# Order of the output projection of a hybrid RWKV-7 / short-convolution block: M2 behind M1, one M1 block through a projection buffer, P4 among the second half's M1, sums and forms spread, end reordered

## The chip, the cores and the metric

The kernel runs on one core of one Trainium2 chip. A core has TensorE (matrix products; its weight loads are listed apart as PEld), VectorE (DVE), ScalarE (ACT), GpSimd (POOL) and SyncE (SP, which here only starts transfers), and 16 DMA engines between HBM and the core's SBUF. The metric is the device time of one execution in microseconds (us). The time before is the median of three runs, 1017.98 us (1017.09 to 1019.04).

## The reference

Inputs are `x` (512 rows of 2048), 16 meta rows put ahead of it, and weights. One layer:

```python
hn = _rmsnorm(h_res, norm_in_g[l])
P = hn @ w_in[l]                         # 2048 -> 4224 + 4096 columns
...
y = _rwkv7_recurrence(rh, decay, kh, vh, kk, kk * ah)     # 16 heads x 64, in chunks of 64 rows
y_a = (yn + bonus.reshape(bsz, L, D_RWKV)) * jax.nn.silu(g_r)
y_b = Bg * _causal_depthwise_conv(Cg * hc, conv_w[l]) * jax.nn.silu(g_c)
mix = jnp.concatenate([y_a, y_b], axis=-1)                # 1024 + 1024 columns
h_res = h_res + mix @ w_out[l]                            # 2048 x 2048
out = _rmsnorm(h_res, norm_f_g)
return out[:, N_META:]
```

The change is in the last three lines: the product of `mix` with `w_out`, the addition of `x` and the final RMSNorm.

## The kernel before

**Stages.** The input projection (L319 to L340) fills TensorE for most of the span; between its matmuls stand the chunk matrices of the recurrence, the recurrence itself (`recur`, L939) and the elementwise work. All products are made in three passes of a high and a low part (`hi`, `lo`): each float32 operand is split, ScalarE casting `hi` and VectorE (for some weights GpSimd) subtracting to get `lo`.

**Output product.** `mix` (four tiles `mix[0..3]` of 128 x 4 x 512, transposed) times `w_out` is computed in two halves of the output's columns. In each half a 2 x 2 block scheme in the manner of Strassen and Winograd makes seven products, named M1, M2, M7, Q6, P5, P4 and M3, in place of eight. Their left operands are parts of `mix` (M1: `mix` of the RWKV half and the first 256 rows, M2: the convolution half and the first 256 rows, P4: the convolution half and the last 256 rows) or *forms* S1, S3, S4, S5 of sums (L1112 `sums(q)`: four operations of 128 x 1024 on VectorE, for q = 0 and 1; L1155 `split_form`: the split of one form, a cast and a subtraction of 128 x 1024; eight of them). Their right operands are blocks of `w_out` (128 x 1024, 512 KB) or sums of blocks. Each product has four blocks g = 0..3 over the summed dimension.

**Units.** A unit `(half, product, g)` is 12 matmuls of 128 x 512: two row parts `s`, two parts `q` of the block, three passes. `units` (L1164) lists all 56 in TensorE's order, and TensorE follows it by hand. Before the change, each half is: M1 (g 0 to 3), then P5, M7, M3, Q6 for each g, then P4 and M2, interleaved in the first half, M2 last in the second. `split_unit` (L1205) makes a unit's right operand: two casts and two subtractions (tiles `o`, six buffers in the pool tag `w`, so up to three units ahead). After a product's last unit `close` (L1247) adds its PSUM banks to the tiles `xa` (first half) and `xb` (second), which also hold `x`; after Q6 six such additions use an SBUF tile `sh`, and when a tile is final, `squares` on ScalarE makes its part of the sum of squares and `gain` on GpSimd multiplies it by the final gain.

**Loads.** `chain[g]` (tiles `X0..X3`) gets its first `w_out` block by `begin_chain` (L1187) or, for g 0 to 2 of the first half, in the projection's weight stream; other blocks are added onto it by a transfer from GpSimd's queue (`add_by_transfer`, L1198) or by VectorE (`add`, L1201). `request` (L1192) loads one block into one of three `raw` buffers that the projection used for its weights. The tiles of the output stage in pool `pw`, `X3` among them, are available when the projection's memory is released (`ph1.close()`, L1142).

**What sets the order.** `at(u, fn, ...)` (L1279) hangs a helper in front of unit u of the list. On VectorE, ScalarE, GpSimd and SP a scheduler orders the work from there and each engine then runs its list strictly in order; the last part of the program (L1374 on) is ordered by hand on VectorE, ScalarE and GpSimd. SP's transfers leave in SP's order: one that waits for its buffer holds up those behind it. The lists around the change:

```python
for half in range(2):
    units += [(half, "M1", g) for g in range(4)]
    units += [(half, prod, g) for g in range(4) for prod in ("P5", "M7", "M3", "Q6")]
    ends = ("P4", 0), ("P4", 1), ("M2", 0), ("P4", 2), ("M2", 1), ("P4", 3), ("M2", 2), ("M2", 3)
    units += [(half, prod, g) for prod, g in sorted(ends, key=lambda e: half and e[0] == "M2")]
```

**End.** The last product (M2 of the second half) is made as bank `end` for rows 0 to 127 and as two banks of 256 columns for rows 128 to 255. `finish` (L1396) scales rows of a tile and stores them, `row_scale` (L1389) makes the row's factor (with a power on GpSimd), `finish_last` (L1408) scales and stores the last four tiles.

Of the kernel before, what the change touches and what calls it, by code (L numbers as in the profile page):

```python
# [9 lines left out]
F32 = mybir.dt.float32  # L10
# [3 lines left out]
ALU = mybir.AluOpType  # L14
# [63 lines left out]
def hymba_kernel(ctx: ExitStack, tc: tile.TileContext, xt, xtok, front, w_in, w_out, pv, lup, cst, msk, gf, out):  # L78
# [1033 lines left out]
    def sums(q):  # L1112
        a11, a21, a12, a22 = quarter(0, T0, q), quarter(0, T1, q), quarter(1, T0, q), quarter(1, T1, q)
        nc.vector.tensor_tensor(out=a22, in0=a22, in1=a21, op=ALU.subtract)
        nc.vector.tensor_tensor(out=a21, in0=a11, in1=a21, op=ALU.subtract)
        nc.vector.scalar_tensor_tensor(out=a11, in0=a22, scalar=-1.0, in1=a11, op0=ALU.mult, op1=ALU.subtract)
        nc.vector.scalar_tensor_tensor(out=a12, in0=a11, scalar=-1.0, in1=a12, op0=ALU.mult, op1=ALU.subtract)
# [16 lines left out]
    for j in range(NPAIR + 4, KT):  # L1134
# [3 lines left out]
        split_mix(j)  # L1138
    for _ in flow:
        pass  # L1140
    prefetch(len(stream))
    ph1.close()  # L1142
# [21 lines left out]
    units = []  # L1164
    for half in range(2):
        units += [(half, "M1", g) for g in range(4)]
        units += [(half, prod, g) for g in range(4) for prod in ("P5", "M7", "M3", "Q6")]
        ends = ("P4", 0), ("P4", 1), ("M2", 0), ("P4", 2), ("M2", 1), ("P4", 3), ("M2", 2), ("M2", 3)
        units += [(half, prod, g) for prod, g in sorted(ends, key=lambda e: half and e[0] == "M2")]
    U = {unit: u for u, unit in enumerate(units)}  # L1170
    right, straight = {}, {}
# [10 lines left out]
    def rows_of(half, k, col, g):  # L1182
        return w_out[2 * half + col, 4 * k + g]

# [4 lines left out]

    def request(half, k, col, g):  # L1192
        t = wp.tile([P, 1024], F32, tag="raw", name=f"wo{half}{k}{col}{g}", bufs=3)
        state["dma"] = nc.sync.dma_start(t, rows_of(half, k, col, g)).ins
        straight[half, k, col, g] = t

# [320 lines left out]
```

## Time and profile before

| | us |
|---|---|
| median of three runs | 1017.98 (1017.09 to 1019.04) |
| the profiled execution's own time | 1016.83 |
| its span on the page | 1015.1 |
| output stage: first M1 weights to the end of the span | 846.62 to 1015.1 |
| first-half block (P5, M7, M3, Q6) starts | 859.55 |
| second half's first P5 starts | 939.28 |
| first and last store issued | 1001.18 and 1010.72 |

The page gives busy time by engine; since TensorE's row is nearly full throughout, it tells little about what can be saved. More is read from the timeline of one engine: each row is a run of equal instructions (start, time until the last one's end, engine, line, operation, output and input, count), and in brackets the idle time just before it and the event that ended it. PEld rows are used for TensorE because a weight load starts only when its operand is there, and because the recorded ends of matmuls are modelled. In the names of tiles buffer numbers are left out: `o` is a split right operand, `S` a form, `m` a part of `mix`, `w` a split weight of the projection's stream, `wo` a raw `w_out` block, `x` a chain tile.

### The profile page before, as it was taken

What the parts mean: (1) busy time and instruction counts of PE and PEld (TensorE: products, weight loads), DVE (VectorE), ACT (ScalarE), POOL (GpSimd) and SP (SyncE); (2) the same over time, 40 slices, a digit from 0 to 9 for tenths busy, and PEclk for the clock granted to TensorE, in tenths of its full rate; (3) what the DMA queues carried; (4) which work ended last, traced back from release to release, by engine and by line L of the source; (5) the groups of instructions that cost most, each with busy time, mean ns of one, the idle gap of its engine ahead of it and who ended that gap; (6) DMA issues with size and microseconds to landing.
All of it is one profiled execution on the core that took longest, in us unless ns stands there. A gap on an engine that the chain in (4) does not pass through costs nothing.

```text
span 1015.1 us, 23761 instructions
## 1 busy us (share of the span) xinstructions
PE 995.6 (98%) x9723; PEld 913.6 (90%) x9723; DVE 684.3 (67%) x1305; ACT 393.9 (39%) x729; POOL 276.2 (27%) x292
## 2 busy tenths in 40 slices
PE   9999999999999999999999999999999999999996
PEld 8899998999988999998999998889898897787875
DVE  7677955587775568654668654244555697998787
ACT  7553423344323433323434323222222335545453
POOL 0122323233232323222423222223332332015001
PEclk9999999999999999999999999999999999999999
DMA  9525576446664363864273956977673698696754
GB/s 325 158 75 140 127 193 172 120 119 149 160 167 134 100 176 87 220 166 118 83 172 95 222 140 188 342 241 229 220 211 88 196 264 190 171 330 139 174 124 166
DMA packets 185037, 174.83 MB, mean 172 GB/s; under 512 B 121568, under 2 KB 142816, under 8 KB 184416
## 3 DMA queue, kind: packets, MB, share of 16 engines
q1 hardware_dynamic: 182336, 164.40, 56.3%
q0 software_dynamic: 2304, 8.39, 5.0%
q8 instruction: 76, 1.25, 0.5%
q10 hardware_dynamic: 288, 0.52, 0.1%
q14 instruction: 33, 0.27, 0.1%
HBM read 136.92 MB, written 36.35 MB: 171 GB/s over the span
## 4 chain that ended last, share of the span: by engine, by line
PE 55%; DVE 8%; DMA 3%; issue 2%; ACT 1%; SPq 0%; POOL 0%; DVEq 0%; ACTq 0%; POOLq 0%
PE ps_gc L328 8%; PE ps_B L328 7%; PE ps_h L328 7%; PE ps_C L328 6%; PE ps_v L328 5%; PE ps_k L328 5%; PE ps_g L328 4%; PE ps_r L328 4%; DVE o L1213 3%; DMA wo<-in_w_out_dram 2%; PE M L1240 2%; PE zy L1009 1%; PE zs L1005 1%; PE g L680 1%; DVE xb L1221 1%
## 5 line engine op out<-in xcount | busy, mean ns | idle before, releaser
L134 ACT CAST w<-wr 128x512 fp32r<-128x512 f32 x252 | 153.2, 618 | 292.7 <-PE ps_k L328 45.8
L135 POOL TENSOR_TENSOR w<-wr,w 128x512 fp32r<-128x512 f32 x119 | 166.6, 1400 | 362.0 <-ACT w L134 310.6
L135 DVE TENSOR_TENSOR w<-wr,w 128x512 fp32r<-128x512 f32 x133 | 94.3, 715 | 104.7 <-ACT w L134 99.6
L328 PE MATMUL ps_k<-xh,w 128*128 128x256 f32 (+1 forms) x512 | 95.6, 284 | 1.1 <-DVE w L135 1.1
L328 PE MATMUL ps_r<-xh,w 128*128 128x256 f32 (+1 forms) x512 | 95.7, 282 | 0.0
L328 PE MATMUL ps_v<-xh,w 128*128 128x272 f32 (+1 forms) x512 | 95.1, 283 | 0.0
L328 PE MATMUL ps_h<-xh,w 128*128 128x258 f32 (+1 forms) x512 | 94.1, 282 | 0.0
L328 PE MATMUL ps_C<-xh,w 128*128 128x258 f32 (+1 forms) x512 | 93.2, 281 | 0.0
L328 PE MATMUL ps_g<-xh,w 128*128 128x258 f32 (+1 forms) x512 | 92.2, 281 | 0.0
L328 PE MATMUL ps_B<-xh,w 128*128 128x512 f32 x256 | 83.4, 394 | 0.0
L328 PEld LDWEIGHTS ps_k<-xh,w 128*128 128x128 f32 x512 | 80.5, 190 | 1.6 <-DVE w L135 1.4
L328 PE MATMUL ps_gc<-xh,w 128*128 128x512 f32 x256 | 81.4, 393 | 0.3 <-DVE w L135 0.3
L328 PEld LDWEIGHTS ps_r<-xh,w 128*128 128x128 f32 x512 | 80.5, 189 | 0.2
L328 PEld LDWEIGHTS ps_h<-xh,w 128*128 128x128 f32 x512 | 79.7, 189 | 0.7
L328 PEld LDWEIGHTS ps_v<-xh,w 128*128 128x128 f32 x512 | 80.1, 189 | 0.3
L328 PEld LDWEIGHTS ps_C<-xh,w 128*128 128x128 f32 x512 | 79.6, 189 | 0.6
L328 PEld LDWEIGHTS ps_g<-xh,w 128*128 128x128 f32 x512 | 79.4, 189 | 0.5
L328 PE MATMUL ps_k<-xl,w 128*128 128x272 f32 (+1 forms) x256 | 73.1, 286 | 0.0
L328 PE MATMUL ps_h<-xl,w 128*128 128x256 f32 (+1 forms) x256 | 72.0, 281 | 0.6 <-issue 0.6
L328 PE MATMUL ps_v<-xl,w 128*128 128x256 f32 (+1 forms) x256 | 72.5, 283 | 0.0
L328 PE MATMUL ps_r<-xl,w 128*128 128x256 f32 (+1 forms) x256 | 72.3, 282 | 0.0
L328 PE MATMUL ps_g<-xl,w 128*128 128x256 f32 (+1 forms) x256 | 72.2, 282 | 0.0
(321 smaller groups left out, 2278.0 us busy)
## 6 DMA issues: line engine op xcount, KB each, us to landing
wr<-in_w_in_dram SPq DMA_DIRECT2D x126, 512.0 KB
ct<-opd SPq DMA_DIRECT2D x64, 288.0 KB
wo<-in_w_out_dram SPq DMA_DIRECT2D x24, 512.0 KB
x<-in_w_out_dram POOLq DMA_DIRECT2D x16, 512.0 KB, 6.2
opd<-ar SPq DMA_DIRECT2D x8, 576.0 KB
opd<-gt SPq DMA_DIRECT2D x16, 288.0 KB
opd<-bt SPq DMA_DIRECT2D x64, 64.0 KB
x<-in_w_out_dram SPq DMA_DIRECT2D x8, 512.0 KB
```

The lines of the kernel that those rows point to most:

```text
L134: nc.scalar.copy(hi, rq)
L135: low[q] = eng.tensor_tensor(out=lo, in0=rq, in1=hi.bitcast(F32), op=ALU.subtract).ins
L328: nc.tensor.matmul(ps[r], ww[:, w], xx[:, kt, a:b], start=(kt == 0 and n == 0), stop=(kt == KT - 1 and n == 2))
L680: nc.tensor.matmul(z[h][:, c - c0], bk[hs, c, h : h + 2, :].rearrange("p a s -> p (a s)"), ar[hs, c].rearrange("p a s -> p (a s)"), start= ...
L1005: nc.tensor.matmul(d[hs, j], w, x[hs], start=(a == 0), stop=(a == b - 1))
L1009: nc.tensor.matmul(d[ho, j], t[hs, o : o + CH], x[hs], start=(a == 0), stop=(a == b - 1))
L1213: nc.vector.tensor_tensor(out=lo, in0=rq, in1=hi.bitcast(F32), op=ALU.subtract)
L1221: nc.vector.tensor_tensor(out=h, in0=h, in1=ps, op=op)
L1240: nc.tensor.matmul(bank[s], left(prod, jj, m, s), w, start=(jj == 0 and n == 0), stop=(jj == 7 and n == 2))
```

## The change

The list of units becomes: half 0's M1 and then M2 (units 0 to 7); the block P5, M7, M3, Q6 four times (8 to 23); P4 g 0 to 2, then the second half's M1 g 0, P4 g 3, M1 g 1 to 3 (24 to 31); the second half's block (32 to 47); its P4 and M2 (48 to 55). The number of units and matmuls is the same. `request` moves ahead of `ph1.close()`, and M1's fourth block of the first half is requested there into a `raw` buffer; its chain tile is loaded later, for its other uses. The forms and sums hang on other units, `sums(1)` now as four separate operations. In the end part one `finish` of tile (0, 3) goes behind the last addition and one `gain` of a quarter behind `row_scale`.

```diff
@@ sums, before ph1.close() @@
-    def sums(q):
+    def sums(q, which=range(4)):
...
+        for n in which:
+            if n < 2:
+                o, x = ((a22, a22), (a21, a11))[n]
+                nc.vector.tensor_tensor(out=o, in0=x, in1=a21, op=ALU.subtract)
+            else:
+                o, x = ((a11, a22), (a12, a11))[n - 2]
+                nc.vector.scalar_tensor_tensor(out=o, in0=x, scalar=-1.0, in1=o, op0=ALU.mult, op1=ALU.subtract)
...
     prefetch(len(stream))
+    straight = {}
+    request(0, 0, 0, 3)
     ph1.close()
@@ units @@
+    def block(half):
+        return [(half, prod, g) for g in range(4) for prod in ("P5", "M7", "M3", "Q6")]
+
+    units = [(0, prod, g) for prod in ("M1", "M2") for g in range(4)] + block(0)
+    units += [(0, "P4", 0), (0, "P4", 1), (0, "P4", 2), (1, "M1", 0), (0, "P4", 3)]
+    units += [(1, "M1", g) for g in range(1, 4)] + block(1) + [(1, prod, g) for prod in ("P4", "M2") for g in range(4)]
@@ what hangs on which unit @@
+    at(0, split_unit, (0, "M1", 3), passing(0, 0, 0, 3))
+    at(2, begin_chain, 0, 3)
     for half in range(2):
-        o = 28 * half
         for g in range(4):
-            b = o + 4 + 4 * g
-            if half == 0:
-                if g == 3:
-                    at(-1, begin_chain, 0, g)
-                    at(0, split_unit, (0, "M1", g), chained(g))
-            else:
-                at(o + g - 4, begin_chain, 1, g)
-                at(o + g - 2, split_unit, (1, "M1", g), chained(g))
-            at(max(o + g, b - 5), add_by_transfer, half, 0, 1, g)
+            b, m1, m2 = U[half, "P5", g], U[half, "M1", g], U[half, "M2", g]
+            if half:
+                at(m1 - 4, begin_chain, 1, g)
+                at(m1 - 2, split_unit, (1, "M1", g), chained(g))
+            at(max(m1 + (half == 0 and g == 3), b - 5), add_by_transfer, half, 0, 1, g)
...
-            if half == 0:
-                at(U[half, "M2", g] - 4, request, 0, 1, 0, g)
-                at(U[half, "M2", g] - 2, split_unit, (0, "M2", g), passing(0, 1, 0, g))
+            if half:
+                at(m2 + 2 * g - g - 11, load_home, g)
             else:
-                at(o + 13 + 2 * g, load_home, g)
+                at(m2 - 5, request, 0, 1, 0, g)
+                at(m2 - 2, split_unit, (0, "M2", g), passing(0, 1, 0, g))
     for n, f in enumerate(("S1", "S3", "S4", "S5")):
-        at(n, split_form, f, 0)
-        if n == 2:
-            at(n + 1, sums, 1)
-        at(6 + n, split_form, f, 1)
+        at((1, 2, 4, 5)[n], split_form, f, 0)
+        at(6 + n, sums, 1, (n,))
+        at((10, 11, 13, 14)[n], split_form, f, 1)
@@ end @@
             squares(1, 2, part)
-            gain(1, 2, nc.vector, cols)
             if part == 0:
-                finish(0, (2, 0, 3))
+                gain(1, 2, nc.vector, cols)
+                finish(0, (2, 0))
                 nc.vector.tensor_tensor(out=fv[:, 1, 0:1], in0=fv[:, 1, 0:1], in1=ssq[:, 1, 3:4], op=ALU.add)
+        finish(0, (3,))
         row_scale(1, 4, nc.vector)
+        gain(1, 2, nc.vector, slice(256, 512))
         finish_last(1)
```

How the instructions stand is settled by a scheduler, so the lists of three places are shown. In the names, `o3_0` is part 0 of unit 3's right operand, `wo0103` the raw block of half 0, second row group, first column group, g 3; `x03` is the chain tile of half 0, g 3; `S101` the low part of form S1 for q = 0.

VectorE where the first half of the output begins, from the last split of `mix` on; before:

```order
L1114 TENSOR_TENSOR mix3_10658<-mix3_10658,mix1_10656 128x4x256
L1160 TENSOR_TENSOR S101_11293<-mix2_10657,S100_11292 128x1024
L1160 TENSOR_TENSOR S301_11289<-mix0_10655,S300_11288 128x1024
L1213 TENSOR_TENSOR o3_0_11315<-x03_11312,o3_0_11315 128x512
L1213 TENSOR_TENSOR o3_1_11318<-x03_11312,o3_1_11318 128x512
L1213 TENSOR_TENSOR o4_0_11353<-x00_11134,o4_0_11353 128x512
L1213 TENSOR_TENSOR o4_1_11356<-x00_11134,o4_1_11356 128x512
L1160 TENSOR_TENSOR S401_11295<-mix2_10657,S400_11294 128x1024
L1213 TENSOR_TENSOR o5_0_11376<-wo0010_11308,o5_0_11376 128x512
L1213 TENSOR_TENSOR o5_1_11379<-wo0010_11308,o5_1_11379 128x512
L1115 TENSOR_TENSOR mix1_10656<-mix1_10656 128x4x256
```

and with the change:

```order
L1215 TENSOR_TENSOR o3_0_11312<-wo0003_11275,o3_0_11312 128x512
L1215 TENSOR_TENSOR o3_1_11315<-wo0003_11275,o3_1_11315 128x512
L1117 TENSOR_TENSOR mix3_10658<-mix3_10658,mix1_10656 128x4x256
L1173 TENSOR_TENSOR S101_11295<-mix2_10657,S100_11294 128x1024
L1215 TENSOR_TENSOR o4_0_11354<-wo0100_11310,o4_0_11354 128x512
L1215 TENSOR_TENSOR o4_1_11357<-wo0100_11310,o4_1_11357 128x512
L1173 TENSOR_TENSOR S301_11291<-mix0_10655,S300_11290 128x1024
L1173 TENSOR_TENSOR S401_11297<-mix2_10657,S400_11296 128x1024
L1215 TENSOR_TENSOR o5_0_11381<-wo0101_11318,o5_0_11381 128x512
L1215 TENSOR_TENSOR o5_1_11384<-wo0101_11318,o5_1_11384 128x512
L1215 TENSOR_TENSOR o6_0_11399<-wo0102_11335,o6_0_11399 128x512
L1215 TENSOR_TENSOR o6_1_11402<-wo0102_11335,o6_1_11402 128x512
```

M1's fourth block (`o3`) comes from a raw buffer and stands ahead of the first sum; the units behind it are M2's (`o4` to `o7`), and P5's first split moves far back.

GpSimd from the first half's block to the second half's first additions by transfer; before:

```order
L1199 DMA x03_11312<-in_w_out_dram 128x1024
L1298 TENSOR_TENSOR xa2_11306<-xa2_11306,gfb_11612 128x512
L1298 TENSOR_TENSOR xa0_11304<-xa0_11304,gfb_11612 128x512
L1298 TENSOR_TENSOR xa3_11307<-xa3_11307,gfb_11612 128x512
L1298 TENSOR_TENSOR xa1_11305<-xa1_11305,gfb_11612 128x512
L1298 TENSOR_TENSOR xa2_11306<-xa2_11306,gfb_11612 128x512
L1199 DMA x10_11858<-in_w_out_dram 128x1024
L1298 TENSOR_TENSOR xa3_11307<-xa3_11307,gfb_11612 128x512
L1199 DMA x11_11878<-in_w_out_dram 128x1024
```

and with the change:

```order
L1300 TENSOR_TENSOR xa0_11306<-xa0_11306,gfb_11620 128x512
L1300 TENSOR_TENSOR xa1_11307<-xa1_11307,gfb_11620 128x512
L1201 DMA x02_11136<-in_w_out_dram 128x1024
L1201 DMA x03_11352<-in_w_out_dram 128x1024
L1201 DMA x10_11824<-in_w_out_dram 128x1024
L1300 TENSOR_TENSOR xa2_11308<-xa2_11308,gfb_11620 128x512
L1300 TENSOR_TENSOR xa0_11306<-xa0_11306,gfb_11620 128x512
L1300 TENSOR_TENSOR xa3_11309<-xa3_11309,gfb_11620 128x512
L1201 DMA x11_11870<-in_w_out_dram 128x1024
L1300 TENSOR_TENSOR xa1_11307<-xa1_11307,gfb_11620 128x512
```

Two gains (`xa0`, `xa1`, whose first quarters are final after M2) now stand ahead of the transfers for g 2 and 3; the other gains stand around the second half's first transfers.

VectorE at the end, from the gain of the first 256 columns of the last bank on; before:

```order
L1298 TENSOR_TENSOR xb0_11778<-xb0_11778,gfb_11612 128x256
L1402 SCALAR_TENSOR_TENSOR xb0_11778<-xb0_11778,fv_11287,gfb_11612 128x512
L1402 SCALAR_TENSOR_TENSOR xb1_11800<-xb1_11800,fv_11287,gfb_11612 128x512
L1451 TENSOR_TENSOR fv_11287<-fv_11287,ssq_11286 128x1
L1446 TENSOR_TENSOR xb0_11778<-xb0_11778,end1_12544 128x256
L1298 TENSOR_TENSOR xb0_11778<-xb0_11778,gfb_11612 128x256
L1392 TENSOR_SCALAR fv_11287<-ssq_11286,fv_11287 128x1
```

and with the change:

```order
L1300 TENSOR_TENSOR xb0_11779<-xb0_11779,gfb_11620 128x256
L1400 SCALAR_TENSOR_TENSOR xb0_11779<-xb0_11779,fv_11289,gfb_11620 128x512
L1449 TENSOR_TENSOR fv_11289<-fv_11289,ssq_11288 128x1
L1444 TENSOR_TENSOR xb0_11779<-xb0_11779,end1_12546 128x256
L1400 SCALAR_TENSOR_TENSOR xb1_11804<-xb1_11804,fv_11289,gfb_11620 128x512
L1390 TENSOR_SCALAR fv_11289<-ssq_11288,fv_11289 128x1
L1300 TENSOR_TENSOR xb0_11779<-xb0_11779,gfb_11620 128x256
```

One scaled tile (`xb1`) moves behind the last bank's addition (`end1`), and the last quarter's gain behind the sum for the row's factor.

More of the change, by code (lines that the diff above doesn't have):

```diff
@@ L1138, in hymba_kernel, with rows_of, request @@
         split_mix(j)
+    def rows_of(half, k, col, g):
+        return w_out[2 * half + col, 4 * k + g]
+    def request(half, k, col, g):
+        t = wp.tile([P, 1024], F32, tag="raw", name=f"wo{half}{k}{col}{g}", bufs=3)
+        state["dma"] = nc.sync.dma_start(t, rows_of(half, k, col, g)).ins
+        straight[half, k, col, g] = t
     for _ in flow:
@@ L1180, in left @@
         return parts[NPAIR + jj][part][:, w][:, tk]
-    def rows_of(half, k, col, g):
-        return w_out[2 * half + col, 4 * k + g]
     def begin_chain(half, g):
@@ L1190, in begin_chain @@
         nc.sync.dma_start(chain[g], rows_of(half, 0, 0, g))
[L1192 to L1195, printed above, removed]
     def add_by_transfer(half, k, col, g):
```

12 lines of the change are left out of this document (1 added, 11 removed).

## The prediction

> **What bounds the kernel now.** I read the page first, then the weight-load queue of TensorE in order of time, because its starts show when each unit of work could begin.
>
> ```profile
> span 1015.1 us, 23761 instructions
> PE 995.6 (98%) x9723; PEld 913.6 (90%) x9723; DVE 684.3 (67%) x1305; ACT 393.9 (39%) x729; POOL 276.2 (27%) x292
> ```
>
> TensorE is busy 98% of the span, and the diff takes away no matmul. So only two things can be won: time in which TensorE waits, and time after its last matmul. The PEld timeline of the output stage has both.
>
> ```profile
> 846.62 8.13 PEld L1240 LDWEIGHTS M<-w,m 128*128 128x128 f32 x36
> 856.40 0.19 PEld L1240 LDWEIGHTS M<-o,m 128*128 128x128 f32 x1 [1.65 <-ACT o L1212]
> 857.13 2.38 PEld L1240 LDWEIGHTS M<-o,m 128*128 128x128 f32 x11 [0.54 <-DVE o L1213]
> ...
> 867.02 1.68 PEld L1240 LDWEIGHTS M<-o,S 128*128 128x128 f32 x8 [1.15 <-DVE o L1213]
> ...
> 869.96 2.36 PEld L1240 LDWEIGHTS Q<-o,S 128*128 128x128 f32 x11 [0.88 <-DVE o L1213]
> ...
> 875.77 5.09 PEld L1240 LDWEIGHTS M<-o,S 128*128 128x128 f32 x23 [0.51 <-DVE o L1213]
> 880.90 2.68 PEld L1240 LDWEIGHTS Q<-o,S 128*128 128x128 f32 x12
> ...
> 905.38 5.40 PEld L1240 LDWEIGHTS P<-o,m 128*128 128x128 f32 x24
> ...
> 931.49 2.62 PEld L1240 LDWEIGHTS M<-o,m 128*128 128x128 f32 x12 [0.67 <-DVE o L1213]
> 934.84 4.41 PEld L1240 LDWEIGHTS M<-o,m 128*128 128x128 f32 x20 [0.73 <-DVE o L1213]
> 939.28 2.68 PEld L1240 LDWEIGHTS P<-o,S 128*128 128x128 f32 x12
> ...
> 974.64 2.91 PEld L1240 LDWEIGHTS M<-o,S 128*128 128x128 f32 x13
> ...
> 989.81 5.10 PEld L1240 LDWEIGHTS P<-o,m 128*128 128x128 f32 x23 [0.66 <-DVE o L1213]
> 994.94 5.40 PEld L1240 LDWEIGHTS end<-home,m 128*128 128x128 f32 x24
> 1000.38 5.93 PEld L1442 LDWEIGHTS end<-home,m 128*128 128x128 f32 x48
> ```
>
> A unit is 12 matmuls. From 880.90 to 905.38 nine of them run without a wait: 24.48 us, 2.72 each. With this the lost time is counted by difference, which is safer than adding bracketed idle times. **A**, the head of the first half: 846.62 to 880.90 holds 11 units (29.92) and takes 34.28, so 4.36 is lost. **B**, between the halves: 905.38 to 939.28 holds 12 (32.64) and takes 33.90: 1.26 lost. **C**, 939.28 to 974.64: 13 units, 35.36, nothing lost. **D**, 974.64 to 1000.38: 9 units' worth (24.48) in 25.74: 1.26 lost. The sum is 6.9 us. **E**, the tail, runs from the last weight load (1000.38 + 5.93 = 1006.31; its matmul takes some 0.2 more) to 1015.1.
>
> Why A waits shows in the chain of waits (start, duration), in VectorE's timeline and, for the price of ScalarE's cast, in the groups of instructions:
>
> ```profile
> 849.99 5.64 DMA x<-in_w_out_dram
> ...
> 968.96 6.22 DMA wo<-in_w_out_dram
> ```
> ```profile
> 856.38 2.50 DVE L1213 TENSOR_TENSOR o<-x,o 128x512 fp32r<-128x512 f32 x4 [1.54 <-ACT o L1212]
> 858.80 1.22 DVE L1160 TENSOR_TENSOR S<-mix,S 128x1024 fp32r<-128x1024 f32 x1
> ...
> 861.14 1.22 DVE L1115 TENSOR_TENSOR mix<-mix 128x1024 f32<-128x1024 f32 x1
> 862.27 1.22 DVE L1160 TENSOR_TENSOR S<-mix,S 128x1024 fp32r<-128x1024 f32 x1
> ```
> ```profile
> L1212 ACT CAST o<-wo 128x512 fp32r<-128x512 f32 x40 | 23.5, 619 | 19.7 <-DVE wo L1203 9.3 <-PE Q L1240 4.1 <-PE M L1240 3.1
> ```
>
> The fourth M1 block is requested only when the projection's memory is free, lands at 855.63, and costs 856.40 − 854.78 + 0.50 = 2.1 us. Then VectorE, back to back from 856.38 (the chain of waits runs through it up to 875.7), is late with later operands: the other 2.3. A 512-wide operation follows the one before it after 0.60 us (2.42 for four), a 1024-wide one after 1.13 (861.14 to 862.27).
>
> **A, part by part.** The fourth M1 block now comes through a projection buffer, requested before the stage. It replaces a request in the same place of SP's queue, so it costs the projection nothing; the chain tile is loaded later, one load of 512 KB more, under units that need other data. M2's four units stand behind M1. They add to VectorE's head work eight splits and two additions, ten operations, 6.0 us; they push P5 back by 4 × 2.72 = 10.9, and the 1.54 us for which VectorE sat idle at 854.8 is used. So VectorE gains 6.4 us on TensorE, where it was 2.3 late. I checked this along the new order, one operation after another by the distances above, with ScalarE's cast (0.62) ahead of each split. M1 g3 is ready at 852.4 (needed 854.8), M2 g0 to g3 at 855.9, 859.4, 860.6, 863.5 (857.5, 860.2, 862.9, 865.7), P5 g0 866.4 (868.4), M7 g0 869.9 (871.1), Q6 g0 875.8 (876.6), M7 g1 881.9 (882.0). Nothing is late, though the last margins are thin. Spreading the sums and forms moves the same 12 operations; the walk has them in their new places.
>
> The loads: three raw buffers carry M1 g3 and M2 in turn, so M2 g2 is requested when M1 g3 is split (852.5), M2 g3 after M2 g0 (855.9), M7's pair at 859.4 and 860.6. With a landing of 6.22, the longest in the chain, M2 g3 lands at 862.1 and the pair at 866.8, where the additions start at 866.4: 0.4 late inside M7 g0's 1.2 us.
>
> What remains is GpSimd. Its multiplications by the final gain take VectorE's time, as GpSimd's timeline, the additions of one kind (shortest/median/longest, ns) and VectorE's timeline show:
>
> ```profile
> 912.58 1.78 POOL L1298 TENSOR_TENSOR xa<-xa,gfb 128x512 f32<-128x512 f32 x1 [11.71 <-ACT sqj_None L1227]
> ...
> 924.52 1.29 POOL L1298 TENSOR_TENSOR xa<-xa,gfb 128x512 f32<-128x512 f32 x1 [3.85 <-ACT sqj_None L1227]
> ```
> ```profile
> L1221 DVE TENSOR_TENSOR xa<-xa,sh x6: 679/686/1789, 910.1 to 916.5; 128x512 f32<-128x512 f32 x6
> ```
> ```profile
> 912.51 4.70 DVE L1221 TENSOR_TENSOR xa<-xa,sh 128x512 f32<-128x512 f32 x4
> 917.13 2.39 DVE L1213 TENSOR_TENSOR o<-x,o 128x512 fp32r<-128x512 f32 x2
> ```
>
> An addition that meets one takes 1.79 instead of 0.69: 1.1 us for each gain. M2's early end lets two gains (x-rows 0 and 1, first quarter) start as soon as the gain vector has landed (asked for at 882.4 in the walk, behind M3 g2's block; 1 MB, so about 888), when VectorE prepares M7 g2 with 1.4 us to spare: 2 × 1.1 − 1.4 = 0.8. I take 0.6 for this and thin margins; bounds 0 and 2.4. **A gives 4.36 − 0.6 = 3.8** (2.0 to 4.36).
>
> **B.** Without M2 here, the DMA requests for the second half go out earlier. Walked likewise, VectorE has M1' g0 ready at 917.6 (TensorE needs it at 920.1) and comes to the first split of P4 g3 at 919.4. From there to P5' g0 it has 16 operations and one 1024-wide addition, 10.7 us, and must be done by 934.6 (32 units and a short start after 846.62): 4.5 to spare. But now six gains fall here, behind the Q6 additions and P4. If five meet two-operand work, 5.5 − 4.5 = 1.0 is lost; six lose 2.1; three, nothing. Locally M1' g1 has only 2.3 us when the first three gains come. I take a loss of 1.5, nearer the upper end, since almost all operations there read two operands as in the rows above. **B gives 1.26 − 1.5 = −0.2** (−0.9 to +1.26).
>
> The Trainium skill, "SBUF — State Buffer", section "SBUF: two separate sides", calls the port pair that VectorE and GpSimd share an exclusive lock held for a whole instruction; 1.79 against 0.69 agrees. By that rule with all six gains at the 1.29 us of the row at 924.52, B would lose 7.7 − 4.5 = 3.2, and the time would be 1.7 us above my sum.
>
> **C and D.** The order on VectorE, ACT and SP from M7' g1 on is the same, as are the times of the last loads against the units; D's 1.26 comes from loads into the freed forms (6.22 at 968.96). I take 0, bounds ±0.5: VectorE may arrive later or earlier by what B leaves.
>
> **E.**
>
> ```profile
> 1005.71 1.41 DVE L1402 SCALAR_TENSOR_TENSOR xb<-xb,fv,gfb 128x512 f32<-128x512 f32 x2
> ...
> 1007.11 0.41 DVE L1446 TENSOR_TENSOR xb<-xb,end 128x256 f32<-128x256 f32 x1
> ...
> 1008.15 0.42 DVE L1298 TENSOR_TENSOR xb<-xb,gfb 128x256 f32<-128x256 f32 x1 [0.63 <-ACT sqj L1227]
> 1008.50 0.21 DVE L1392 TENSOR_SCALAR fv<-ssq,fv 128x1 f32<-128x1 f32 x1
> ...
> 1009.36 0.49 DVE L1411 TENSOR_SCALAR xb<-xb,fv 128x512 f32<-128x512 f32 x1 [0.66 <-POOL fv L98]
> ```
> ```profile
> 1009.00:1010.00 1.00, 0.00 (x0) 0.00 (x0) 0.64 (x2) 0.64 (x1) 0.90 (x2) 1.00 1.01 385
> 1010.00:1011.00 1.00, 0.00 (x0) 0.00 (x0) 0.69 (x1) 0.09 (x1) 0.41 (x1) 0.77 0.38 139
> 1011.00:1012.00 1.00, 0.00 (x0) 0.00 (x0) 0.00 (x0) 0.00 (x0) 0.00 (x0) 0.50 1.01 375
> ```
>
> These are VectorE's last operations and, below, busy times by stage (the last two columns are DMA share and GB/s). TensorE is done by about 1006.5, but the last addition waits for VectorE until 1007.11; one of the two L1402 now follows it: 0.55 sooner. The quarter's gain leaves the place ahead of L1392: 0.35 less, minus a little for the L1402 now in between. The last scale comes 0.8 sooner. The stores run at 385 GB/s and pause near 1010 at 139 GB/s, (385 − 139) / 385 = 0.64 us of missing flow; only this can close, so **E gives 0.65** (0.3 to 0.85).
>
> **Sum.** 3.8 − 0.2 + 0 + 0.65 = 4.25. Against the profiled execution's 1016.83 (its span of 1015.1 and 1.7 around it) this is 1012.6; the median of the runs shown is 1.15 higher, so I predict 1017.98 − 4.25 = **1013.7**. The bounds add up to gains of 0.9 and 7.0: 1017.1 to 1011.0.
>
> **Rivals.** (1) *All of it*: the gains meet TensorE-fed additions or idle moments, A and B lose nothing: 4.36 + 1.26 + 0.65 = 6.3, 1011.7. For it: the median of 0.686 among those six additions, most of which ran freely while gains were about. Against: the thin margins. (2) *The stall moves*: VectorE stays the bound, A keeps 2.4 us of waits and B loses 0.9 more than now: 2.0 − 0.9 + 0.65 = 1.75, 1016.2. For it: VectorE's 1.79 rows. (3) *Slower*: M2's blocks come late. Behind 852.5 five transfers of 0.52 MB must land (M2 g2, g3, M7's pair, an x block), and the fourth chain tile's adding transfer now falls among them.
>
> ```profile
> 847.00:852.00 5.00, 5.00 (x24) 4.13 (x23) 4.11 (x6) 3.29 (x5) 0.87 (x1) 1.00 0.68 107
> 852.00:857.00 5.00, 3.67 (x16) 2.47 (x14) 3.46 (x5) 2.70 (x5) 0.00 (x0) 1.00 1.02 350
> ```
>
> While such a transfer ran (issued 848.74) the engines moved 107 GB/s; at that rate 2.62 MB take 24.5 us, the pair is there at 877.0, M7 g0 starts near 880.1 instead of 871.1, and 9.0 − 4.36 − 0.65 = 4.0 is lost: 1022. It stalls below 169 GB/s and turns slower below about 128. Against it: the next five microseconds moved 350. (4) *Nothing happens*: the order could have been settled elsewhere; the instruction order shows M2 and the tail moved on their engines, so I give this no share.
>
> **Chances.** Forecast (a gain of 2.5 to 5.5) 0.53, rival 1 0.22, rival 2 0.16, rival 3 0.07, anything else slower 0.02. A measurement here can tell about 0.2%, 2.0 us, from no change. Faster by more: 0.53 + 0.22 + 0.05 of rival 2's upper part = 0.80; within: 0.11; slower: 0.09. The range is 1011.2 to 1016.9; the forecast's own is 1012.4 to 1015.4.
>
> **What would show it.** Right: no wait of over 0.3 us at M1 g3 or in the units up to M3 g1 (a span of 41 us for 15 units); short waits where gains run, near M7 g2 and M1' g1 to P5' g0; D still losing 1.2; stores without a pause. Wrong: PEld waiting on a DMA-fed cast in M2 or M7 g0 (rival 3), waits on VectorE's splits of over 3 us in A and B together beyond D (rival 2), or a matmul that takes longer than its 0.227 us share of a unit.

## The result and the profile after

| | before | changed |
|---|---|---|
| median, first comparison | 1017.43 us (1016.21 to 1019.79, 14 runs) | 1015.10 us (1012.01 to 1018.27, 14 runs) |
| ratio with 95% interval | | 0.9973 [0.9960, 0.9985] |
| median, second comparison | 1018.11 us (1015.57 to 1019.95, 19 runs) | 1014.72 us (1013.56 to 1016.07, 8 runs) |
| ratio with 95% interval | | 0.9968 [0.9957, 0.9979] |
| profiled execution, its span | 1016.83, 1015.1 us | 1014.59, 1012.8 us |

The kernel became faster by 2.3 to 3.4 us; 4.25 were forecast. 1015.1 lies in the range, 1.4 above the forecast of 1013.7. The page of the changed kernel reads as before in its shares (span, and busy time by engine):

```profile
span 1012.8 us, 23757 instructions
PE 995.8 (98%) x9723; PEld 914.3 (90%) x9723; DVE 684.7 (68%) x1305; ACT 393.2 (39%) x729; POOL 282.0 (28%) x292
```

What changed shows in TensorE's weight loads (PEld timeline of the changed kernel: start, time to the end of the last, engine, line, operation, operands, count, idle time ahead and its releaser):

```profile
848.17 8.13 PEld L1242 LDWEIGHTS M<-w,m 128*128 128x128 f32 x36
856.34 13.56 PEld L1242 LDWEIGHTS M<-o,m 128*128 128x128 f32 x60
...
927.06 2.91 PEld L1242 LDWEIGHTS M<-o,m 128*128 128x128 f32 x13
930.80 3.33 PEld L1242 LDWEIGHTS M<-o,m 128*128 128x128 f32 x15 [0.83 <-DVE o L1215]
934.75 1.69 PEld L1242 LDWEIGHTS M<-o,m 128*128 128x128 f32 x8 [0.62 <-DVE o L1215]
...
972.12 2.68 PEld L1242 LDWEIGHTS M<-o,S 128*128 128x128 f32 x12
975.40 0.19 PEld L1242 LDWEIGHTS M<-o,S 128*128 128x128 f32 x1 [0.59 <-ACT o L1214]
976.29 2.37 PEld L1242 LDWEIGHTS M<-o,S 128*128 128x128 f32 x11 [0.70 <-DVE o L1215]
...
988.29 5.11 PEld L1242 LDWEIGHTS P<-o,m 128*128 128x128 f32 x23 [0.68 <-DVE o L1215]
993.44 5.40 PEld L1242 LDWEIGHTS end<-home,m 128*128 128x128 f32 x24
998.88 5.93 PEld L1440 LDWEIGHTS end<-home,m 128*128 128x128 f32 x48
```

The waits at the head are gone: from 848.17 to 927.06 stand 29 units at 2.72, 78.88 us, and the stretch takes 78.89. Waits for split operands remain between the halves (930.80, 934.75, and 0.42 at 945.25) and in the last quarter (975.40 to 988.29). The output stage, from its first weight load to the span's end, takes 1012.8 − 848.17 = 164.7 us instead of 168.45. But it starts 1.55 us later than before, at the end of the projection, where the change only has one block requested early; this comes up with the sum and in the last section.

The tail after the last weight load is shorter as forecast. VectorE's last operations in the changed kernel, and its stages of 1 us (busy time of PE, PEld, DVE, ACT, POOL, the granted clock, DMA share, GB/s):

```profile
1005.05 0.42 DVE L1444 TENSOR_TENSOR xb<-xb,end 128x256 f32<-128x256 f32 x1
1005.39 0.75 DVE L1400 SCALAR_TENSOR_TENSOR xb<-xb,fv,gfb 128x512 f32<-128x512 f32 x1
...
1007.10 0.49 DVE L1409 TENSOR_SCALAR xb<-xb,fv 128x512 f32<-128x512 f32 x1 [0.44 <-POOL fv L98]
```
```profile
1006.00:1007.00 1.00, 0.00 (x0) 0.00 (x0) 0.66 (x3) 0.07 (x1) 0.60 (x1) 1.00 1.05 422
1007.00:1008.00 1.00, 0.00 (x0) 0.00 (x0) 0.91 (x2) 0.72 (x1) 0.90 (x2) 1.00 0.98 369
1008.00:1009.00 1.00, 0.00 (x0) 0.00 (x0) 0.42 (x1) 0.00 (x0) 0.14 (x1) 0.63 1.00 375
```

The last addition starts 0.24 us after TensorE's last weight load ends (998.88 + 5.93 = 1004.81), and the last scale 2.05 behind it. The pause of the stores, 139 GB/s for 1 us before, has closed.

### The profile page after: what moved, and what is told of

The parts are those of the page before. It is cut to its first block, busy times and chain, and to the rows that moved or that the text cites. A ratio compares the mean times of both kernels' runs of the same rounds, so it can differ in the third digit from the quotient of the medians.

```text
span 1012.8 us, 23757 instructions
## 1 busy us (share of the span) xinstructions
PE 995.8 (98%) x9723; PEld 914.3 (90%) x9723; DVE 684.7 (68%) x1305; ACT 393.2 (39%) x729; POOL 282.0 (28%) x292
## 4 chain that ended last, share of the span: by engine, by line
PE 53%; DVE 10%; DMA 3%; issue 3%; ACT 1%; SPq 0%; POOL 0%; DVEq 0%; ACTq 0%; POOLq 0%
PE ps_gc L328 8%; PE ps_B L328 7%; PE ps_h L328 7%; PE ps_C L328 6%; PE ps_v L328 5%; PE ps_k L328 5%; PE ps_g L328 5%; PE ps_r L328 4%; DVE o L1215 4%; DMA wo<-in_w_out_dram 3%; DVE xa L1223 1%; PE zy L1009 1%; PE zs L1005 1%; PE g L680 1%; DVE xb L1223 1%
```

## The experiments

Medians of one kernel differ by up to 0.8 us between groups of runs (the kernel before: 1017.42 to 1018.23). The stage's length inside a trace repeated within 0.6 us in the three kernels that were traced twice, where the span moved by 0.8 to 1.2, so it is the main measure. The table has, worked out from the weight loads' starts as in the prediction, the time lost beyond 2.72 us a unit in units 0 to 19 (head), 20 to 39 (between) and 40 to 53 (last), and the time from the end of the last weight load to the span's end (tail). "Changed" is the run of the result, "after_again" the same kernel once more.

| kernel | stage | head | between | last | tail | ratio to before |
|---|---|---|---|---|---|---|
| before | 168.45 | 4.36 | 1.26 | 1.26 | 8.75 | |
| before_again | 168.82 | 4.14 | 1.26 | 1.87 | 8.74 | |
| changed | 164.66 | 0.01 | 1.55 | 2.27 | 8.02 | 0.9973 [0.9960, 0.9985] |
| after_again | 164.07 | 0.01 | 1.43 | 1.81 | 8.01 | 0.9968 [0.9957, 0.9979] |
| old_tail | 164.51 | 0.01 | 1.48 | 1.51 | 8.70 | 0.9973 [0.9957, 0.9988] |
| m2_back | 164.44 | 0.88 | 0.98 | 1.69 | 8.08 | 0.9962 [0.9948, 0.9976] |
| m1_only | 166.27 | 2.59 | 1.29 | 1.62 | 7.97 | 0.9983 [0.9973, 0.9993] |
| spread_only | 166.96 | 3.35 | 1.11 | 1.35 | 8.36 | 0.9983 [0.9973, 0.9993] |
| no_gains | 163.31 | 2.62 | 0.00 | 0.00 | 7.88 | 0.9934 [0.9921, 0.9947] |
| gains_gap | 164.19 | 1.44 | 0.00 | 1.66 | 8.27 | 0.9950 [0.9938, 0.9963] |
| acc_only | 165.50 | 0.01 | 1.43 | 3.20 | 8.05 | 0.9959 [0.9946, 0.9973] |
| gains_acc | 161.75 | 0.01 | 0.00 | 0.87 | 8.07 | 0.9937 [0.9925, 0.9948] |
| gains_acc_again | 161.75 | 0.01 | 0.00 | 1.01 | 7.92 | 0.9934 [0.9922, 0.9946] |
| m2_gap | 162.47 | 0.04 | 0.00 | 1.67 | 7.95 | 0.9938 [0.9924, 0.9952] |

### Both kernels once more

The kernels unedited.

> The changed kernel once more. In its first profile the output stage (first M1 weights to the end of the span) takes 164.6 us against 168.5 before, 3.9 less, but it begins 1.55 us later, so that the span is only 2.3 less. Theory 1, chance: the later start comes from a short stretch of half-speed matmuls near 306 us and a wait near 637 us, in code that the change does not touch. Then the stage takes 164.6 +- 0.5 again, the start moves by a microsecond or more from run to run, and over many runs the difference to before comes to 3 to 4 us. Theory 2, the change itself delays the start: the stage again begins near 848.2 and the difference stays near 2.3.

> The kernel before, looked at a second time, since the whole accounting starts from one trace of it. If that trace was typical, the stage is again 168 to 169 us, with 4.0 to 4.7 us lost at the head of the first half, 1.0 to 1.5 between the halves and 1.0 to 1.5 in the last quarter of the second half; other places or sums would mean that the terms of the prediction were read from an odd execution.

Stage 164.07 for the changed kernel and 168.82 for the one before: 4.75 us apart, where the first two traces gave 3.8. The terms were not read from an odd execution, but the last quarter of the kernel before lost 1.87 this time, above the 1.5 that was expected. The changed kernel's stage began at 847.96, again near 848.2, as theory 2 has it. The other traces speak against that theory: in the five with the early request and without the half-speed stretch near 306 us the stage begins at 846.7 in the mean (846.62 before), in the six with both at 848.2 (848.1 in the two with the stretch and without the request, before_again and spread_only).

### The gains left out

```diff
-        at(30 + 2 * n, gain, n // 2, n % 2, nc.gpsimd)
+        pass
```

> The changed kernel without the eight GpSimd multiplications of the first half's tiles by the final gain (that part of the result is left out). Theory 1: the waits between the halves (1.28 us) and the longer waits before the last product (2.28 us against 1.26 before) come from VectorE being held by these gains, the second because the raw-buffer transfers then start late. Then the first fall to 0.3 or less, the second to 1.0 or less, and the time is 2.0 to 2.5 us below the changed kernel's. Rival: VectorE is too loaded there whatever GpSimd does; then both waits stay within 0.4 us and the time within 0.5.

Every wait between the halves and in the last quarter disappeared. So these come from GpSimd's multiplications. The median was 1011.33 us, 3.4 below the changed kernel's beside it (1014.72), more than the 2.0 to 2.5 expected. The changed kernel's timelines show the gains meeting VectorE's work (VectorE, then GpSimd):

```profile
890.68 1.21 DVE L1205 TENSOR_TENSOR wo<-wo,wo 128x1024 f32<-128x1024 f32 x1
...
892.95 2.49 DVE L1215 TENSOR_TENSOR o<-wo,o 128x512 fp32r<-128x512 f32 x4
...
920.59 4.69 DVE L1223 TENSOR_TENSOR xa<-xa,sh 128x512 f32<-128x512 f32 x4
925.20 2.38 DVE L1215 TENSOR_TENSOR o<-x,o 128x512 fp32r<-128x512 f32 x2
...
928.64 2.71 DVE L1215 TENSOR_TENSOR o<-x,o 128x512 fp32r<-128x512 f32 x2
...
935.94 2.52 DVE L1205 TENSOR_TENSOR x<-x,wo 128x1024 f32<-128x1024 f32 x1
```
```profile
890.02 9.02 POOL L1300 TENSOR_TENSOR xa<-xa,gfb 128x512 f32<-128x512 f32 x2 [0.39 <-DMA gfb<-in_gf_dram]
...
920.65 1.78 POOL L1300 TENSOR_TENSOR xa<-xa,gfb 128x512 f32<-128x512 f32 x1 [1.14 <-ACT sqj_None L1229]
922.73 1.40 POOL L1300 TENSOR_TENSOR xa<-xa,gfb 128x512 f32<-128x512 f32 x1 [0.30 <-ACT sqj_None L1229]
925.56 1.47 POOL L1300 TENSOR_TENSOR xa<-xa,gfb 128x512 f32<-128x512 f32 x1 [1.43 <-ACT sqj_None L1229]
...
935.73 1.64 POOL L1300 TENSOR_TENSOR xa<-xa,gfb 128x512 f32<-128x512 f32 x1
```

Four additions take 4.69 beside two gains; in a kernel whose gains stand elsewhere (gains_acc, below) the same four take 2.49, so 1.1 for each. The addition at 935.94 takes 2.52 instead of 1.23.

But a wait appeared at the head, 2.62 us, which nobody had put there (PEld of no_gains, then a row of its chain of waits, then one of GpSimd's):

```profile
866.57 0.53 PEld L1242 LDWEIGHTS M<-o,m 128*128 128x128 f32 x3 [0.38 <-DVE o L1215]
867.77 1.68 PEld L1242 LDWEIGHTS M<-o,m 128*128 128x128 f32 x8 [0.67 <-DVE o L1215]
```
```profile
856.35 8.72 DMA wo<-in_w_out_dram
```
```profile
856.54 0.89 POOL L1201 DMA_DIRECT2D x<-in_w_out_dram  x1 [6.60 <-DVE o L1215]
```

The load of M2's fourth block took 8.72 us to land, with the adding transfer of the fourth chain tile issued 0.19 behind it: the place of rival 3. In what follows this is called the race at the head: two transfers start almost together, and how far apart seems to decide whether the load lands late. In the changed kernel (chain of waits, GpSimd) the distance was 0.55, and the load took 5.43:

```profile
857.56 5.43 DMA wo<-in_w_out_dram
```
```profile
858.11 0.89 POOL L1201 DMA_DIRECT2D x<-in_w_out_dram  x1 [6.96 <-ACT S L1172]
```

### The end in its former order

```diff
             squares(1, 2, part)
+            gain(1, 2, nc.vector, cols)
             if part == 0:
-                gain(1, 2, nc.vector, cols)
-                finish(0, (2, 0))
+                finish(0, (2, 0, 3))
...
-        finish(0, (3,))
         row_scale(1, 4, nc.vector)
-        gain(1, 2, nc.vector, slice(256, 512))
```

> The changed kernel with the end part in the order of before. Theory: the tail (last weight load to the end of the span) goes from 7.99 back to 8.8 us, with the pause in the stores near 3.5 us ahead of the end, and the rest of the stage stays; 0.8 us slower than the changed kernel. Rival: the stores' rate alone sets the tail; then it is 0.2 us or less.

The tail is 8.70 instead of 8.02 and 8.01: the new end is worth 0.69 us, with nothing else moved. The medians cannot tell 0.7 us apart (1014.28 here, 1014.72 for the changed kernel beside it).

### M2 back behind P4

```diff
-    units = [(0, prod, g) for prod in ("M1", "M2") for g in range(4)] + block(0)
-    units += [(0, "P4", 0), (0, "P4", 1), (0, "P4", 2), (1, "M1", 0), (0, "P4", 3)]
-    units += [(1, "M1", g) for g in range(1, 4)] + block(1) + ...
+    units = [(0, "M1", g) for g in range(4)] + block(0)
+    units += [(0, p, g) for p, g in (("P4", 0), ("P4", 1), ("M2", 0), ("P4", 2), ("M2", 1), ("P4", 3), ("M2", 2), ("M2", 3))]
+    units += [(1, "M1", g) for g in range(4)] + block(1) + ...
```

> The changed kernel with the first half's M2 back among its P4 and the second half's M1 behind both, as before; M1's fourth block still through the projection buffer, the sums, forms and the end as changed. Theory: the wait at M1 g3 (2.1 us) stays away, but VectorE is late again for P5, M7 and Q6, so the stage's first 11 units lose 2 us or more and the waits between the halves are near 1.3: 2 us or more slower than the changed kernel. Rival: the fourth M1 block and the spreading were enough; then the first 11 units lose under 0.7 us.

The stage is as long as the changed kernel's, 164.44, and the first 15 units lose nothing although P5 follows M1 at once: the rival came, not the theory. The head loses 0.85 in unit 15 alone, where Q6 g2 waits for forms (PEld row below): they hang on units 10 to 14, chosen for a list with four more units in front.

```profile
889.95 2.14 PEld L1242 LDWEIGHTS Q<-o,S 128*128 128x128 f32 x10 [0.98 <-DVE S L1173]
```

### The two other parts, each alone

m1_only is m2_back with the old places of forms and sums:

```diff
-        at((1, 2, 4, 5)[n], split_form, f, 0)
-        at(6 + n, sums, 1, (n,))
-        at((10, 11, 13, 14)[n], split_form, f, 1)
+        at(n, split_form, f, 0)
+        if n == 2:
+            at(n + 1, sums, 1)
+        at(6 + n, split_form, f, 1)
```

spread_only is m2_back with M1's fourth block through its chain tile:

```diff
-    request(0, 0, 0, 3)
...
-    at(0, split_unit, (0, "M1", 3), passing(0, 0, 0, 3))
-    at(2, begin_chain, 0, 3)
+    at(-1, begin_chain, 0, 3)
+    at(0, split_unit, (0, "M1", 3), chained(3))
```

> Of the change only two parts: the fourth M1 block through a projection buffer, and the new end. M2's units stand behind the first half's P4, and the left sums and forms where they were before. Nothing is left out. If the block's late request costs 2.1 us and VectorE's lateness behind it 2.3 us as two separate things (my step), the head of the first half still loses about 2.3 us. If VectorE was late only because it had to wait for that block (rival), it loses 0.5 us or less.

> Of the change only the spreading of the left sums and forms, and the new end. The fourth M1 block comes through its chain tile, requested when the projection's memory is free, and M2's units stand behind the first half's P4. Nothing is left out. If block and lateness are two separate things (my step), the wait at M1 g3 stays, about 1.6 to 2.1 us, and of the other 2.3 us nothing or little is left. If spreading does nothing by itself (rival), the head loses 4 us or more as before.

Weight loads of m1_only, then of spread_only:

```profile
865.09 0.53 PEld L1242 LDWEIGHTS M<-o,S 128*128 128x128 f32 x3 [0.39 <-DVE o L1215]
866.82 1.68 PEld L1242 LDWEIGHTS M<-o,S 128*128 128x128 f32 x8 [1.21 <-DVE o L1215]
...
869.75 2.37 PEld L1242 LDWEIGHTS Q<-o,S 128*128 128x128 f32 x11 [0.88 <-DVE o L1215]
```
```profile
858.82 0.19 PEld L1241 LDWEIGHTS M<-o,m 128*128 128x128 f32 x1 [1.85 <-ACT o L1213]
859.54 2.39 PEld L1241 LDWEIGHTS M<-o,m 128*128 128x128 f32 x11 [0.54 <-DVE o L1214]
...
893.52 1.46 PEld L1241 LDWEIGHTS Q<-o,S 128*128 128x128 f32 x7 [0.93 <-DVE S L1172]
```

They are two separate things. Without the spreading the block's wait is gone and VectorE's lateness stays, 2.59. With the spreading alone the wait for the block stays, 2.25 in units 2 and 3, and the rest of the 3.35 is the forms' late place again.

### The gains in VectorE's gaps, and the adding transfer held back

gains_gap lets six gains wait until VectorE stands idle between transfers in the second half:

```diff
+    def paced(k, unit, ts):
+        lo = right[unit, 1][1]
+        ins = nc.gpsimd.tensor_copy(out=tick[:, k : k + 1], in_=lo[:, 511:512].bitcast(F32)).ins
+        with tc.issue_after(ins):
+            for t, n in ts:
+                gain(t, n, nc.gpsimd)
...
-    for n in range(8):
-        at(30 + 2 * n, gain, n // 2, n % 2, nc.gpsimd)
+    for t in range(2):
+        at(30 + 4 * t, gain, t, 0, nc.gpsimd)
+    for k, (prod, g, ts) in enumerate(
+        (("M3", 1, ((2, 1), (0, 1))), ("M3", 2, ((3, 1), (1, 1))), ("M7", 3, ((2, 0), (3, 0))))
+    ):
+        at(U[1, prod, g] - 2, paced, k, (1, prod, g), ts)
```

gains_acc has this and holds the adding transfer back in the same way; acc_only has only the second:

```diff
-            at(max(m1 + (half == 0 and g == 3), b - 5), add_by_transfer, half, 0, 1, g)
+            if (half, g) != (0, 3):
+                at(max(m1, b - 5), add_by_transfer, half, 0, 1, g)
...
+    def add_late():
+        lo = right[(0, "M7", 0), 1][1]
+        ins = nc.gpsimd.tensor_copy(out=tick[:, 3:4], in_=lo[:, 511:512].bitcast(F32)).ins
+        with tc.issue_after(ins):
+            add_by_transfer(0, 0, 1, 3)
+
+    at(8, add_late)
```

> The changed kernel, with six of the eight multiplications by the final gain moved: each pair waits for a tiny GpSimd copy that reads an operand which VectorE makes in the second half's block (M3' g1, M3' g2, M7' g3), where VectorE idles between transfers; the other two stay early. Nothing is left out. If the gains are what holds VectorE between the halves and what makes it late afterwards (theory 1), the waits between the halves fall from 1.3 us to 0.3 or less, the waits in the last quarter of the second half from 2.3 us to about 1.0, and the output stage is 2 us shorter than the changed kernel's 164.1 to 164.7: about 162. If the gains cost VectorE the same wherever they stand (rival), the 1.1 us for each turns up as waits near M3' g1 to M7' g3 and the stage stays within 0.7 us of 164.4.

> As the run before (gains moved into VectorE's gaps), and besides the adding transfer of the fourth chain tile is held back until VectorE has split M7 g0, so that M2's fourth block and M7's pair land without it. Nothing is left out. If the adding transfer beside M2's fourth block is a race that costs only when it is lost (my theory), the block lands within 5.5 us, the first 20 units lose nothing, and the stage is as in the run before, about 162, or 2.6 us below it if that one loses the race. If the held-back transfer is now late for P5 g3 (rival), a wait of 1 us or more stands there (unit 20), and the stage is longer than the run before.

> The changed kernel with one edit: the adding transfer of the fourth chain tile held back until VectorE has split M7 g0. Nothing is left out. In the traces of the changed kernel that transfer was issued 0.29 to 0.55 us behind the load of M2's fourth block, and the block landed in time; where it was issued 0.07 and 0.19 us behind, the block was 2 to 3 us late. If this is a race (my theory), this trace is like the changed kernel's, a stage of 164.1 to 164.7 with the waits between the halves (1.3 us) and at the end (2.3 us) left as they are, and the timed runs reach less far up than the changed kernel's 1018.3. If holding it back moves the time by itself (rival), the stage leaves that range by over 0.7 us.

> The kernel with the six gains in VectorE's gaps and the adding transfer held back, again, on the chip of the other runs of this group. Nothing is left out. The stage should be within 0.5 us of 161.75, with waits of no more than 1.2 us in all, and the median near 1010.7; a stage near 164 would mean that the earlier trace was a lucky one.

With the gains moved nothing is lost between the halves. gains_gap's stage was no shorter for it, since it lost the race at the head (chain of waits, GpSimd; distance 0.07), and its last quarter lost 1.66, not the 1.0 expected:

```profile
858.36 7.51 DMA wo<-in_w_out_dram
```
```profile
858.43 0.89 POOL L1201 DMA_DIRECT2D x<-in_w_out_dram  x1 [6.48 <-DVE o L1215]
```

gains_acc takes both away (PEld; GpSimd's moved gains), and was the shortest of all, twice:

```profile
856.55 13.56 PEld L1242 LDWEIGHTS M<-o,m 128*128 128x128 f32 x60
...
927.27 8.12 PEld L1242 LDWEIGHTS M<-o,m 128*128 128x128 f32 x36
...
970.79 5.40 PEld L1242 LDWEIGHTS M<-o,S 128*128 128x128 f32 x24
...
979.57 5.34 PEld L1242 LDWEIGHTS P<-o,m 128*128 128x128 f32 x24 [0.40 <-DVE o L1215]
985.58 5.08 PEld L1242 LDWEIGHTS P<-o,m 128*128 128x128 f32 x23 [0.67 <-DVE o L1215]
```
```profile
948.29 3.52 POOL L1300 TENSOR_TENSOR xa<-xa,gfb 128x512 f32<-128x512 f32 x2
...
959.17 2.54 POOL L1300 TENSOR_TENSOR xa<-xa,gfb 128x512 f32<-128x512 f32 x2
...
969.08 2.53 POOL L1300 TENSOR_TENSOR xa<-xa,gfb 128x512 f32<-128x512 f32 x2
```

Its medians were 1010.69 and 1011.46 us, 0.9937 and 0.9934 of the kernel before, against 0.9973 and 0.9968 for the change as it was: 3 to 4 us better.

acc_only missed its expectation: head and between are the changed kernel's, but the last quarter lost 3.20 and the stage was 165.5, 0.8 above the range, which is the sign that was set for the rival. Its timed runs do not bear the rival out: the median of 1013.63 (1012.94 to 1016.29) lies below the changed kernel's 1014.72 and 1015.10, and the intervals overlap. What holding the transfer back does alone stays open.

### M2 behind P4, with the gains moved

m2_gap is m2_back with gains_gap's edit, and `(8, 9, 11, 12)` for `(10, 11, 13, 14)`.

> M2's units behind the first half's P4 as before, the fourth M1 block through a projection buffer, the sums and forms spread (the second half's forms two units earlier than in the change, since four units fewer stand ahead of them), the new end, and six gains moved into VectorE's gaps. No adding transfer falls among M2's loads here. Nothing is left out. If moving M2 is worth nothing by itself (what the runs so far suggest), head and end lose nothing and the stage is within 0.7 us of 161.75, the stage of the run with M2 in front, the gains moved and the adding transfer held back. If M2 in front gives VectorE room that it needs (my step), the head loses 1 us or more again and the stage is 163 or longer.

Head and between lose nothing. The stage is 0.72 above 161.75, just outside the 0.7 that was set, and all of it is in the last quarter. The ratio to before, 0.9938, is that of the kernels with M2 in front (0.9937 and 0.9934): M2's move is worth nothing that the medians can tell.

### What the last quarter waits for

The rows of the last transfer in the chain of waits are quoted for the changed kernel, acc_only, gains_acc and m2_gap in turn; that of before (968.96, 6.22) stands in the prediction.

```profile
967.60 6.06 DMA wo<-in_w_out_dram
```
```profile
965.41 6.54 DMA wo<-in_w_out_dram
```
```profile
965.23 5.71 DMA wo<-in_w_out_dram
```
```profile
963.39 6.49 DMA wo<-in_w_out_dram
```

| | unit of the second half's M7 g3 starts | transfer lands | later by | lost in the last quarter |
|---|---|---|---|---|
| gains_acc | 970.79 | 970.94 | 0.15 | 0.87 |
| before | 974.64 | 975.18 | 0.54 | 1.26 |
| m2_gap | 968.95 | 969.88 | 0.93 | 1.67 |
| changed | 972.12 | 973.66 | 1.54 | 2.27 |
| acc_only | 969.51 | 971.95 | 2.44 | 3.20 |

The loss is 0.7 to 0.8 us more than the lateness of this one landing, in every row, and in eight of the other nine traces too; in the ninth, no_gains, the block lands 0.8 ahead of the unit and nothing is lost. Its block goes into `home`, and its cast stands on ScalarE ahead of M3 g3's, for which TensorE waits. Both when the transfer starts and how long it takes matter. It starts when VectorE has emptied a buffer that an earlier transfer filled, so lateness of VectorE between the halves can be handed on through the transfers. The issue stood 5.24 to 5.68 us ahead of M7 g3's unit in the five traces with M2 behind P4 and the gains early, 4.10 to 5.05 in the four with M2 in front and the gains early, and 5.56 in all four with the gains moved. How long the transfer takes varied from 5.71 to 6.56 in these thirteen, for reasons that the runs do not show. m2_gap's 0.72 is this: the same issue, 5.56 ahead of M7 g3's unit (968.95 − 963.39) as in gains_acc (970.79 − 965.23), and a landing 0.78 slower.

## Why the prediction was right, and where not

**A, the head: 3.8 forecast, 4.35 gained.** That 4.36 us would go was right, in its two portions: the block's late landing (4.36 − 2.59 = 1.8 by m1_only, 2.25 still there in spread_only; 2.1 forecast) and VectorE's lateness (2.59 left in m1_only; 2.3 forecast). The cause given for the second did not hold up: that M2's four units "push P5 back" is not needed. m2_gap has P5 right behind M1 and loses 0.04. The spreading of the sums and forms is enough, which the prediction counted as moving the same operations and gave no worth of its own. Whether M2's move would have been enough without the spreading, no run shows; with it, the move bought looser places for the forms.

The 0.6 held back for GpSimd's two early gains did not come: there VectorE kept its pace (890.68 and 892.95: 1.21 and four in 2.49; one addition at 898.41 took 1.71 instead of 1.23) and GpSimd waited (890.02: 9.02 us for two, 2.53 for two at 969.08 of gains_acc). The Trainium skill, "SBUF — State Buffer", section "SBUF: two separate sides", gives the shared ports to whichever instruction starts first. Both sides of that are in this trace, GpSimd shut out at 890.02 and VectorE held up at 920.59; which side it would be, the prediction had no row to tell.

**B, between the halves: a loss of 0.2 forecast, 0.3 and 0.2 found** (1.26 before; 1.55 and 1.43 now). The mechanism is shown: without the gains, or with six of them elsewhere, nothing is lost here. Of the losses found, 0.28 and 0.17 stand in the stretch called C, forecast at 0. The size owes something to luck: the 934.6 in the prediction's sum is 0.9 later than 846.62 + 32 × 2.72 = 933.66, and "a short start" does not account for it; with 933.66 five gains would have cost 1.9 instead of 1.0.

**D, the last quarter: 0 forecast; this is the step that failed in the profiled pair**, 1.26 before and 2.27 now; the second pair, 1.87 and 1.81, shows no loss. The prediction named the transfer at 968.96 as the source of the 1.26, but took the times of the last loads against the units as unchanged. They did change: the issue stood 5.68 and 5.24 us ahead of M7 g3's unit before, 4.52 and 5.00 now. All four traces with M2 in front and the gains early have it late, and lose 2.2 in the mean (1.5 to 3.2); the five with M2 behind and the gains early lose 1.6 (1.3 to 1.9). So some 0.6 of the 1.0 goes with M2 in front, and the rest is scatter between executions.

**E, the tail: 0.65 forecast, 0.73 gained**, 0.69 with old_tail.

**The sum.** The stage became 3.8 us shorter in the first pair of traces and 4.75 in the second, 4.3 in the mean, where 4.25 was forecast. That this is so close is in part luck: in the mean of the two pairs A gave 0.4 more than forecast and D 0.5 less. That the medians fell by only 2.3 and 3.4 can have two reasons that the traces show; how much of each was in the timed runs they do not show. The projection ended later in both traces of the changed kernel (848.17 and 847.96; 846.62 and 847.45 before), 1.0 later in the mean, for the most part through the clock (below): both have the half-speed stretch, before has it in one of two. And the race at the head was lost in two of the five traces of kernels with M2 in front and the adding transfer not held back, at 1.4 and 2.6 us each. How often it is lost in the timed runs, which leave no trace, stays open; the two traced executions that lost it were the longest of their kernels' runs (1012.04 of no_gains, 1014.92 of gains_gap).

**The signs and the rivals.** Of the signs set for being right, the head without waits, waits from M1' g1 to P5' g0 and stores without a pause came; the waits near M7 g2 and D at 1.2 did not. Rival 1 (all of it) had A and E right and B wrong, where the gains do meet VectorE's work. Rival 2 (VectorE stays the bound) did not happen at the head. Rival 3 named the place and the neighbour of the one danger that was real. Its price was wrong: not 107 GB/s for all that must land, but one load that landed 2 to 3 us later, in the two traces of these kernels where the adding transfer followed within 0.2 us; neither was slower than the kernel before.

## What to carry to other kernels

A block that several engines prepare is late for separate reasons: take each edit back alone before crediting the one that looks largest. Put GpSimd's elementwise work where VectorE waits for transfers, by a tiny GpSimd instruction that reads what VectorE has just made; here that took away the 1.0 to 1.6 us lost between the halves, more than the new end gave (0.7). Where a transfer that is not urgent can start beside one that is, hold it back, as a good trace does not show a race that another execution loses; here none of the three traces with it held back lost the race, while its worth in time alone stayed open.

## What the runs showed of the hardware

**An adding transfer from GpSimd's queue can hold up a load issued just ahead of it.** For M2's fourth block, at distances of 0.29 (after_again), 0.41 (old_tail) and 0.55 us (changed) the 512 KB load landed in 5.35, 5.07 and 5.43; at 0.19 and 0.07 us (no_gains, gains_gap) it took 8.72 and 7.51. With the adding transfer held back (acc_only, gains_acc, gains_acc_again) it took 4.03, 4.27 and 4.61. Closeness alone is not enough: in m1_only an adding transfer was issued 0.04 us behind another such load (861.05), with no other load issued within 6 us of it, and the load landed in 4.20. What else must be under way stays open, and the distances were not varied on purpose, only as they came.

**TensorE's clock was halved in mid-kernel in some executions.** Near 302 us TensorE waits: in the changed kernel it has only two groups of 32 small transposes between 301.7 and 305.1 us, with 1.97 us idle between them. One window of before, then of before_again, the same program:

```profile
306.00:308.00 2.00, 2.00 (x10) 1.62 (x10) 0.52 (x1) 1.97 (x4) 0.00 (x0) 1.00 0.78 236
```
```profile
306.00:308.00 2.00, 2.00 (x6) 1.57 (x5) 0.69 (x1) 1.03 (x2) 0.84 (x1) 0.50 0.63 241
```

The granted clock (third number from the end) is 1.00 in one and 0.50 in the other. Of the 14 traces 8 have this stretch; their output stage starts at 848.2 in the mean, that of the other six at 846.7. In each of the eight it lasts 3.41 us, so a TensorE that is busy throughout would lose half of that, an estimate of 1.7. So some 1.5 us of a span can come from here and say nothing about an edit. The Trainium skill, "TensorE: Matmul & The Clock Gate", part 1 on the clock gate, describes a half rate after an idle window of about 3.4 us whose phase runs free of the kernel. That one program shows both, and the length of 3.41, agree with it; a whole idle window is not in the trace, where the longest pause was the 1.97.
